# Hybrid decoder trunk on one core: inverse roots per token tile, attention low parts on VectorE, quotients and half sums behind the next piece

## The chip, the cores and the metric

The kernel runs on one core of one Trainium2 chip. The metric is device time in microseconds (us) of one execution, as the median of several runs. A core has five engines, each with an instruction queue of its own that it works off in order: PE (TensorE, the matrix products), DVE (VectorE), ACT (ScalarE), POOL (GpSimd) and SP (which here only issues transfers). An instruction that waits for another engine holds up everything behind it on its own engine.

## The reference

A batch of one, 512 tokens, 1024 channels, float32. Two layers, each followed by a SwiGLU feed-forward block: a recurrent layer (RG-LRU and Mamba-2 heads) and a layer of dilated window attention. The change touches the attention layer alone:

```python
def attention_layer(x, norm_g, w_qkv, q_norm, k_norm, w_out):
    h = rmsnorm(x, norm_g)
    qkv = (h @ w_qkv).reshape(b, l, 3, ATT_HEADS, ATT_HEAD_DIM)      # 16 heads of 64
    q = partial_rope(rmsnorm(qkv[:, :, 0], q_norm), pos) * (ATT_HEAD_DIM ** -0.5)
    k = partial_rope(rmsnorm(qkv[:, :, 1], k_norm), pos)
    v = qkv[:, :, 2]
    for window, dilation in ((128, 1), (512, 4), (2048, 16)):
        o_i, m_i, d_i = dilated_window_attention(q, k, v, window, dilation)   # softmax in a band
        ...
    # the three merged by their denominators
    return x + o @ w_out
```

`rmsnorm` of q and k is over the 64 channels of one head: each head of each token needs the inverse root of a mean square.

## The kernel before

All matrix products take float32 operands as a high part (`wh`, `xh`: rounded to fp32r) and a low part (`wl`, `xl`: what is left), three products each (low by high, high by low, high by high). `split` makes the parts: ACT casts the high part, and another engine subtracts to get the low part, DVE for most weights, POOL for those of the attention (`on_pool`: the 24 tiles of `in_w_qkv` and the 8 of `in_w_ao`). Weights come as 128x1024 tiles through three raw buffers and three pairs of parts, two weights ahead (`weight_emit`, `AHEAD`).

The attention layer works on four groups of four heads. For a group, `qk_pieces` gives 16 pieces of work for PE (4 weight tiles by 4 token tiles of 128, six matmuls each) and `v_pieces` 8 more. Pieces wait in the list `pieces`; `fill_in(n)` issues the next n of them between the small steps of the heads, so that PE has dense work while DVE and ACT prepare the next small step. After every piece, `drain(2)` issues up to two entries of a second list, `queue`: the finishing of q and k.

When the last weight tile of q and k of a token tile is done, `finish_a` copies it out of PSUM (ACT, `q`) and squares it (ACT, `qsq`). Then follow, out of `queue`, a sum over each head (DVE, L766 `qss<-qsq`, one for each token tile); once all four tiles are summed, `finish_b`: mean and epsilon (DVE, L776) and the power -0.5 on POOL for all four tiles in one instruction (L778 `qrs<-qss,mhalf`, 128x32); then `finish_c` four times (DVE, L783 `q<-q,qrs`), and the rotary part (`finish_d`, `finish_e`: `rc`, `rs`, and two sums).

The heads go in eight pairs p. For each pair: `pair_T` transposes q and k on PE and splits them (`qk_hi` ACT, `qk_lo` DVE); `scores(p, b)` for three blocks b multiplies (PE, L866 `ps_s`), adds the mask with a running maximum (DVE, L877 `s<-ps_s,cst`), takes exponentials (ACT, L878), reciprocals of the sums (DVE, L881) and the quotients (POOL, L883 `s<-s,m`); `turn` transposes the quotients (PE, L889 `ps_pT`) and splits them (`ph` ACT, `pl` DVE); `values` multiplies with v (PE, L904 and L905 `ps_o`) and at the end adds the two halves (`bot` ACT L912, `o` DVE L913) and splits `o`. The list `steps` in the loop over p sets how these alternate with pieces; the work of pair p+1's scores lies between the turns and values of pair p. The finishing of q and k of groups 1, 2 and 3 falls into pairs 0, 2 and 4.

PSUM is shared out by two pools: `pa`, four buffers for the pieces (`ps_qkv`, `ps_v`, `ps_ao`), and `pm`, three buffers for `ps_s`, `ps_pT` and `ps_qT`, beside one buffer for `ps_o`. A buffer comes free when ACT and DVE have read it. The final order on each engine is made by a scheduler from the order in the code and from when it expects operands to be ready.

Of the kernel before, what the change touches and what calls it, by code (L numbers as in the profile page):

```python
# [58 lines left out]
def trunk(ctx: ExitStack, tc: tile.TileContext, a):  # L59
# [27 lines left out]
    on_pool = ("in_w_qkv", "in_w_ao")  # L87

    def split(src, hi, lo, eng=V):
        S.copy(hi, src)  # L90
        eng.tensor_tensor(out=lo, in0=src, in1=hi.bitcast(F32), op=ALU.subtract)  # L91
# [11 lines left out]
    def weight_emit(i):  # L103
        while emitted[0] <= min(i, len(specs) - 1):
            j = emitted[0]
            src, n = specs[j]
            raw = wp.tile([P, WMAX], F32, tag="raw", bufs=NRAW, name=f"wr{j}")
            hi = wp.tile([P, WMAX], F32R, tag="whi", bufs=NSPL, name=f"wh{j}")
            lo = wp.tile([P, WMAX], F32R, tag="wlo", bufs=NSPL, name=f"wl{j}")
            step = n if j else n // 4  # L110
            for c in range(0, n, step):
                nc.sync.dma_start(out=raw[:, c:c + step], in_=src[:, c:c + step])
                split(raw[:, c:c + step], hi[:, c:c + step], lo[:, c:c + step], G if src.tensor.name in on_pool else V)
            w_of[j] = (hi, lo)
            emitted[0] += 1
# [575 lines left out]
    with ExitStack() as actx:  # L691
# [36 lines left out]
        def drain(n):  # L728
            for _ in range(min(n, len(queue))):
                queue.pop(0)()  # L730
# [3 lines left out]
        def qk_pieces(g):  # L734
            pss, sqs = [], {}

            def piece(kp, t):
                i = i_qkv[g, kp]
                if t == 0:
                    w_cur[i] = weight_get(i)  # L740
                    if kp == 0:
                        for _ in range(NT):
                            pss.append(pa.tile([P, T], F32, tag="pa", name="ps_qkv"))
                        qk[g] = at.tile([P, NT, 8, 64], F32, tag="q", name="q", bufs=2)
                        sqs["ss"] = am.tile([P, NT, 8], F32, tag="qss", name="qss")
                wh, wl = w_cur[i]
# [8 lines left out]
                if t == 1:  # L755
                    weight_emit(i + AHEAD)
# [3 lines left out]
            def finish_a(t):  # L760
# [5 lines left out]
                queue.append(lambda: V.tensor_reduce(out=sqs["ss"][:, t], in_=sq, axis=AX.X, op=ALU.add))  # L766
                if t == NT - 1:
                    queue.append(finish_b)
                    for u in range(NT):
                        queue.append(lambda u=u: finish_c(u))  # L770
                    queue.append(finish_d)
                    queue.append(finish_e)

            def finish_b():
                ss = sqs["ss"].rearrange("p t h -> p (t h)")
                V.tensor_scalar(out=ss, in0=ss, scalar1=1.0 / 64, scalar2=EPS, op0=ALU.mult, op1=ALU.add)  # L776
                rs = am.tile([P, NT, 8], F32, tag="qrs", name="qrs")
                G.tensor_tensor(out=rs.rearrange("p t h -> p (t h)"), in0=ss, in1=mhalf[:, :NT * 8], op=ALU.pow)  # L778
                sqs["rs"] = rs
# [24 lines left out]
        def v_pieces(g):  # L804
            pss = []

            def piece(vp, t):
# [15 lines left out]
                if t == 1:  # L823
# [33 lines left out]
        def scores(p, b):  # L857
# [23 lines left out]
            V.reciprocal(m[:, 2, :k], m[:, 1, :k])  # L881
            for u, s in enumerate(done):
                G.tensor_scalar(out=s, in0=s, scalar1=m[:, 2, u:u + 1], scalar2=1.0, op0=ALU.mult, op1=ALU.mult)  # L883
# [11 lines left out]
        def values(h, b):  # L895
# [17 lines left out]
            V.tensor_tensor(out=o[rows], in0=po[:64], in1=bot[rows], op=ALU.add)  # L913
            if e == 1:
                hi, lo = slot(8 + p if p < 4 else p - 4, F32R)
                split(o, hi, lo)
                oT.append((hi, lo))
# [25 lines left out]
        def fill_in(n=1):  # L943
            for _ in range(min(n, len(pieces))):
                pieces.pop(0)()
                drain(2)
# [8 lines left out]
        drain(len(queue))  # L955
# [143 lines left out]
```

## Time and profile before

| | |
|---|---|
| median of 3 runs | 1375.89 us (1375.66 to 1377.72) |
| the profiled execution, its own time | 1374.7 us |
| its span in the trace | 1372.9 us |
| PE busy | 1327.4 us, 97% of the span |
| DVE, ACT, POOL busy | 757.1, 554.1, 141.5 us |
| mean granted clock of TensorE | 0.986 |

The span runs from the first to the last instruction. PE is busy nearly all the time, so what counts is where it stands still, and where its granted clock is 0.50 in place of 1.00, which are its two levels of 1.2 and 2.4 GHz. The attention layer lies between about 717 and 1015 us of the span.

### The profile page before, as it was taken

The numbers are of one execution on the slowest core, as the hardware profiler recorded it, in microseconds if no ns is written. First come the engines' busy times: TensorE is split into PE (matmuls) and PEld (weight loads), VectorE is DVE, ScalarE is ACT, GpSimd is POOL, SyncE is SP. The second block draws the span as 40 slices with busy tenths as digits, with TensorE's granted clock in tenths as the row PEclk, the third lists the DMA queues.
The fourth block names the chain that finished last, engine by engine and source line by source line (L and its number), as shares of the span: only waits on it lengthen the run. The fifth ranks groups of instructions, "written<-read, shape, count | busy, mean of one in ns | idle before, by whom it ended". The sixth has DMA issues, their size and how long they took to land.

```text
span 1372.9 us, 15950 instructions
## 1 busy us (share of the span) xinstructions
PE 1327.4 (97%) x6314; PEld 1088.8 (79%) x6314; DVE 757.1 (55%) x1220; ACT 554.1 (40%) x818; POOL 141.5 (10%) x114
## 2 busy tenths in 40 slices
PE   8999989999999999999998889889999999999998
PEld 6877767788888888888887778777788888888887
DVE  7877799875444344444463454556564434444442
ACT  6643867443323223222343445556542322322221
POOL 0000000000000000000025344453300000000000
PEclk9999999999999999999999999989999999999999
DMA  6322223522333233333232211111123333333332
GB/s 234 109 92 77 93 77 109 152 93 92 92 102 98 92 95 101 90 100 106 81 104 93 62 47 62 47 47 47 46 93 105 95 92 96 101 92 98 106 89 81
DMA packets 38556, 126.53 MB, mean 92 GB/s; under 512 B 4289, under 2 KB 5057, under 8 KB 38353
## 3 DMA queue, kind: packets, MB, share of 16 engines
q1 hardware_dynamic: 38480, 125.51, 29.7%
q8 instruction: 49, 0.80, 0.2%
q14 instruction: 27, 0.21, 0.0%
HBM read 123.36 MB, written 2.13 MB: 91 GB/s over the span
## 4 chain that ended last, share of the span: by engine, by line
PE 87%; DVE 5%; ACT 4%; POOL 3%; issue 1%; DMA 0%; SPq 0%; ACTq 0%; POOLq 0%
PE ps_pr L119 24%; PE ps_pr L120 23%; PE ps_pr L121 23%; PE ps_qkv L752 2%; PE ps_qkv L754 2%; PE ps_qkv L753 2%; POOL qrs L778 2%; PE ps_s L866 1%; DVE q L783 1%; PE ps_pT L889 1%; POOL wl L91 1%; PE ps_o L904 1%; ACT wh L90 1%; PE ps_v L820 1%; PE ps_o L905 1%
## 5 line engine op out<-in xcount | busy, mean ns | idle before, releaser
L90 ACT CAST wh<-wr 128x1024 fp32r<-128x1024 f32 (+2 forms) x223 | 228.2, 1024 | 608.7 <-PE ps_pr L121 379.7
L119 PE MATMUL ps_pr<-xh,wl 128*128 128x512 f32 x1056 | 416.4, 394 | 12.3 <-DVE wl L91 12.0
L120 PE MATMUL ps_pr<-xl,wh 128*128 128x512 f32 x1056 | 414.3, 392 | 0.1
L121 PE MATMUL ps_pr<-xh,wh 128*128 128x512 f32 x1056 | 413.1, 391 | 0.0
L91 DVE TENSOR_TENSOR wl<-wr,wh 128x1024 fp32r<-128x1024 f32 (+2 forms) x191 | 225.9, 1184 | 53.6 <-ACT wh L90 53.2
L119 PEld LDWEIGHTS ps_pr<-xh,wl 128*128 128x128 f32 x1056 | 199.3, 189 | 54.9 <-DVE wl L91 12.8
L120 PEld LDWEIGHTS ps_pr<-xl,wh 128*128 128x128 f32 x1056 | 199.4, 189 | 43.6 <-DVE xl L194 2.0
L121 PEld LDWEIGHTS ps_pr<-xh,wh 128*128 128x128 f32 x1056 | 199.2, 189 | 41.7 <-issue 0.7
L120 PE MATMUL ps_pr<-al,wh 128*128 128x512 f32 x352 | 136.9, 389 | 0.0
L121 PE MATMUL ps_pr<-ah,wh 128*128 128x512 f32 x352 | 136.9, 389 | 0.0
L119 PE MATMUL ps_pr<-ah,wl 128*128 128x512 f32 x352 | 136.9, 389 | 0.0
L91 POOL TENSOR_TENSOR wl<-wr,wh 128x1024 fp32r<-128x1024 f32 x32 | 76.7, 2396 | 435.6 <-ACT wh L90 435.6
L673 DVE TENSOR_TENSOR tu<-ps_pr,nrb 128x512 f32<-128x512 f32 x44 | 30.4, 691 | 130.5 <-PE ps_pr L121 130.5
L681 DVE TENSOR_TENSOR x<-ps_pr,x 128x512 f32<-128x512 f32 x48 | 33.2, 692 | 120.1 <-PE ps_pr L121 119.9
L671 DVE TENSOR_TENSOR tg<-ps_pr,nrb 128x512 f32<-128x512 f32 x44 | 30.4, 691 | 94.0 <-PE ps_pr L121 94.0
L120 PEld LDWEIGHTS ps_pr<-al,wh 128*128 128x128 f32 x352 | 66.1, 188 | 13.8
L119 PEld LDWEIGHTS ps_pr<-ah,wl 128*128 128x128 f32 x352 | 66.1, 188 | 13.7
L121 PEld LDWEIGHTS ps_pr<-ah,wh 128*128 128x128 f32 x352 | 66.1, 188 | 13.6
L752 PE MATMUL ps_qkv<-wh,xl 128*128 128x512 f32 x128 | 54.3, 425 | 7.6 <-DVE v L830 7.6
L878 ACT ACTIVATE s<-s,m 128x512 f32<-128x512 f32 (+3 forms) x64 | 35.4, 554 | 54.9 <-DVE m L877 54.9
L754 PE MATMUL ps_qkv<-wh,xh 128*128 128x512 f32 x128 | 50.7, 396 | 0.0
L753 PE MATMUL ps_qkv<-wl,xh 128*128 128x512 f32 x128 | 50.6, 395 | 0.0
(231 smaller groups left out, 1671.0 us busy)
## 6 DMA issues: line engine op xcount, KB each, us to landing
wr<-in_w_gu SPq DMA_DIRECT2D x88, 512.0 KB, 3.5
wr<-in_w_in SPq DMA_DIRECT2D x35, 512.0 KB, 3.5
wr<-in_w_dn SPq DMA_DIRECT2D x32, 448.0 KB, 3.3
wr<-in_w_qkv SPq DMA_DIRECT2D x24, 512.0 KB, 3.5
wr<-in_w_out SPq DMA_DIRECT2D x16, 512.0 KB, 3.5
wr<-in_w_dn SPq DMA_DIRECT2D x16, 512.0 KB, 3.5
x<-in_xT SPq DMA_DIRECT2D x16, 256.0 KB, 3.4
bcs<-csd SPq DMA_DIRECT2D x16, 256.0 KB, 4.6
```

The costliest lines, as they stand in the source:

```text
L90: S.copy(hi, src)
L91: eng.tensor_tensor(out=lo, in0=src, in1=hi.bitcast(F32), op=ALU.subtract)
L119: mm(ps, lhsT=wl[ws], rhs=xh[xs], start=start, stop=False)
L120: mm(ps, lhsT=wh[ws], rhs=xl[xs], start=False, stop=False)
L121: mm(ps, lhsT=wh[ws], rhs=xh[xs], start=False, stop=stop)
L671: V.tensor_tensor(out=tg, in0=pg, in1=rb, op=ALU.mult)
L673: V.tensor_tensor(out=tu, in0=pu, in1=rb, op=ALU.mult)
L681: V.tensor_tensor(out=x[m], in0=ps, in1=x[m], op=ALU.add)
L752: mm(pss[t], lhsT=xl[:, ts_], rhs=wh[:, cols], start=(k == 0), stop=False)
L753: mm(pss[t], lhsT=xh[:, ts_], rhs=wl[:, cols], start=False, stop=False)
L754: mm(pss[t], lhsT=xh[:, ts_], rhs=wh[:, cols], start=False, stop=(k == KD - 1))
L878: S.activation(s, s, AF.Exp, scale=-1.0, bias=m[:, 0, u:u + 1], accum_out=m[:, 1, u:u + 1])
```

## The change

Four edits. (1) The low parts of the attention weights are made by DVE (`on_pool` goes). (2) The finishing of q and k runs by token tile: sum, mean and POOL power for one tile of 128x8, at a count of two pieces from the tile's copy (the tile's own last piece counts), and its use (`finish_c`) four pieces later; a list with counts (`later`, `tick`) takes the place of `queue` and `drain`. (3) Reciprocals and quotients of `scores`, and the half sum with its split in `values`, are put into a list that is issued behind the next piece (`after_piece`). (4) `weight_emit` inside the q, k and v pieces is called at the third token tile in place of the second.

```diff
-    on_pool = ("in_w_qkv", "in_w_ao")
-    def split(src, hi, lo, eng=V):
+    def split(src, hi, lo):
         S.copy(hi, src)
-        eng.tensor_tensor(out=lo, in0=src, in1=hi.bitcast(F32), op=ALU.subtract)
+        V.tensor_tensor(out=lo, in0=src, in1=hi.bitcast(F32), op=ALU.subtract)
...
-        def drain(n):
-            for _ in range(min(n, len(queue))):
-                queue.pop(0)()
+        after_piece = []
+        def later(n, f):
+            queue.append([n, f])
+        def tick():
+            for e in queue:
+                e[0] -= 1
+            due = [e for e in queue if e[0] <= 0]
+            queue[:] = [e for e in queue if e[0] > 0]
+            for _, f in due:
+                f()
...
-                if t == 1:
+                if t == 2:
                     weight_emit(i + AHEAD)
...
-                queue.append(lambda: V.tensor_reduce(out=sqs["ss"][:, t], in_=sq, axis=AX.X, op=ALU.add))
+                later(2, lambda: finish_b(t, sq))
+                later(6, lambda: finish_c(t))
                 if t == NT - 1:
-                    queue.append(finish_b)
-                    for u in range(NT):
-                        queue.append(lambda u=u: finish_c(u))
-                    queue.append(finish_d)
-                    queue.append(finish_e)
+                    later(7, finish_d)
+                    later(8, finish_e)
...
-            def finish_b():
-                ss = sqs["ss"].rearrange("p t h -> p (t h)")
+            def finish_b(t, sq):
+                ss = sqs["ss"][:, t]
+                V.tensor_reduce(out=ss, in_=sq, axis=AX.X, op=ALU.add)
                 V.tensor_scalar(out=ss, in0=ss, scalar1=1.0 / 64, scalar2=EPS, op0=ALU.mult, op1=ALU.add)
-                rs = am.tile([P, NT, 8], F32, tag="qrs", name="qrs")
-                G.tensor_tensor(out=rs.rearrange("p t h -> p (t h)"), in0=ss, in1=mhalf[:, :NT * 8], op=ALU.pow)
-                sqs["rs"] = rs
+                G.tensor_tensor(out=sqs["rs"][:, t], in0=ss, in1=mhalf[:, :8], op=ALU.pow)
...
-            V.reciprocal(m[:, 2, :k], m[:, 1, :k])
-            for u, s in enumerate(done):
-                G.tensor_scalar(out=s, in0=s, scalar1=m[:, 2, u:u + 1], scalar2=1.0, op0=ALU.mult, op1=ALU.mult)
+            def quotients():
+                V.reciprocal(m[:, 2, :k], m[:, 1, :k])
+                for u, s in enumerate(done):
+                    G.tensor_scalar(out=s, in0=s, scalar1=m[:, 2, u:u + 1], scalar2=1.0, op0=ALU.mult, op1=ALU.mult)
+            after_piece.append(quotients)
...
         def fill_in(n=1):
             for _ in range(min(n, len(pieces))):
                 pieces.pop(0)()
-                drain(2)
+                tick()
+            ready = after_piece[:]
+            after_piece.clear()
+            for f in ready:
+                f()
```

The half sum in `values` is wrapped the same way as `quotients` (`add`, with the split of `o` in it). Lines shift: L766, L776, L778 and L783 of before are L784, L785, L786 and L790 of the change, and L91 is L89.

How this moves instructions is seen best on DVE in pair 0, where group 1 of q and k is finished. Names: `qss` sums of squares, `q` the projected tile, `pl` low part of turned weights, `wl` low part of a weight, `o` the half sum, `ISA s,m` the scores' masked maximum. Before, DVE's queue there reads:

```order
L766 TENSOR_REDUCE qss<-qsq 128x8
L846 SCALAR_TENSOR_TENSOR qk_lo<-ps_qT,gain_5363,qk_hi 128x512
L913 TENSOR_TENSOR o<-ps_o,bot 64x512
L766 TENSOR_REDUCE qss<-qsq 128x8
L776 TENSOR_SCALAR qss<-qss 128x32
L91 TENSOR_TENSOR pl<-ps_pT,ph 128x512
L783 TENSOR_TENSOR q<-q,qrs 128x512 x4
L877 ISA s,m<-ps_s,cst 128x512
```

In the change the same stretch, from the second tile on, reads:

```order
L784 TENSOR_REDUCE qss<-qsq 128x8
L853 SCALAR_TENSOR_TENSOR qk_lo<-ps_qT,gain_5363,qk_hi 128x512
L785 TENSOR_SCALAR qss<-qss 128x8
L790 TENSOR_TENSOR q<-q,qrs 128x512
L926 TENSOR_TENSOR o<-ps_o,bot 64x512
L784 TENSOR_REDUCE qss<-qsq 128x8
L785 TENSOR_SCALAR qss<-qss 128x8
L89 TENSOR_TENSOR wl_6036<-wr_6034,wh_6035 128x1024
L89 TENSOR_TENSOR pl<-ps_pT,ph 128x512
L790 TENSOR_TENSOR q<-q,qrs 128x512
L884 ISA s,m<-ps_s,cst 128x512
```

For each tile the product `q<-q,qrs` stands directly behind the `qss<-qss` whose power POOL still has to take (for the last tile one `wl` and one `pl` lie between), and the half sum, `pl` and the scores come behind these. In pairs 2 and 4 the last part reads slightly differently: the `wl` stands ahead of the last `qss<-qss`.

On POOL, the stretch from the first to the second group before (a `wl` is a 128x1024 subtraction, `qrs` the power, `s<-s,m` quotients):

```order
L91 TENSOR_TENSOR wl_5837<-wr_5835,wh_5836 128x1024
L883 TENSOR_SCALAR s<-s,m 128x256 x2
L91 TENSOR_TENSOR wl_5898<-wr_5896,wh_5897 128x1024
L91 TENSOR_TENSOR wl_5997<-wr_5995,wh_5996 128x1024
L778 TENSOR_TENSOR qrs<-qss,mhalf 128x32
L883 TENSOR_SCALAR s<-s,m 128x512 x2
```

and in the change:

```order
L786 TENSOR_TENSOR qrs<-qss,mhalf 128x8 x4
L892 TENSOR_SCALAR s<-s,m 128x512 x2
L892 TENSOR_SCALAR s<-s,m 128x128 x2
L892 TENSOR_SCALAR s<-s,m 128x384 x2
L892 TENSOR_SCALAR s<-s,m 128x256 x2
L786 TENSOR_TENSOR qrs<-qss,mhalf 128x8 x4
```

POOL is left with powers and quotients; the 32 `wl` stand in DVE's queue. Up to pair 4, PE's and ACT's rows are the same as before, and SP's are the same throughout; in pairs 5 to 7 some rows of PE and ACT change places.

## Rows read from the trace of the kernel before

**Rows 1.** The page: engine, busy us (share of the span) and instructions.

```profile
PE 1327.4 (97%) x6314; PEld 1088.8 (79%) x6314; DVE 757.1 (55%) x1220; ACT 554.1 (40%) x818; POOL 141.5 (10%) x114
```

**Rows 2.** Waits of PE, 700 to 1000 us: total us, times, longest.

```profile
PE ps_s L866 <- DVE m L877: 16.5, 3, 5.5
PE ps_qkv L752 <- DVE v L830: 7.6, 1, 7.6
PE ps_o L904 <- DVE pl L91: 2.8, 3, 1.6
PE ps_pT L889 <- POOL s L883: 1.4, 1, 1.4
```

**Rows 3.** Windows behind the stalls: busy us by engine, granted clock, DMA share, GB/s.

```profile
759.12:762.43 3.31, 3.31 (x8) 2.64 (x9) 1.12 (x3) 0.00 (x0) 0.00 (x0) 0.50 0.00 0
803.76:810.20 6.44, 6.30 (x30) 5.67 (x31) 5.17 (x18) 5.47 (x15) 4.50 (x5) 0.50 0.02 4
...
922.36:929.60 7.24, 7.10 (x33) 6.47 (x34) 5.20 (x18) 5.82 (x16) 5.30 (x6) 0.50 0.02 6
sum 21.76, PE 21.33 PEld 18.79 DVE 16.01 ACT 15.58 POOL 12.62; mean PE 5.33 PEld 4.70 DVE 4.00 ACT 3.89 POOL 3.16
```

**Rows 4.** Timeline of POOL in pair 0: start, us, instruction.

```profile
792.78 2.39 POOL L91 TENSOR_TENSOR wl<-wr,wh 128x1024 fp32r<-128x1024 f32 x1 [7.79 <-ACT wh L90]
795.13 5.44 POOL L778 TENSOR_TENSOR qrs<-qss,mhalf 128x32 f32<-128x32 f32 x1
```

**Rows 5.** Timeline of DVE in pair 0.

```profile
789.54 0.74 DVE L846 SCALAR_TENSOR_TENSOR qk_lo<-ps_qT,gain,qk_hi 128x512 fp32r<-128x512 f32 x1
791.87 0.67 DVE L766 TENSOR_REDUCE qss<-qsq 128x8 f32<-128x512 f32 x1
792.57 0.18 DVE L776 TENSOR_SCALAR qss<-qss 128x32 f32<-128x32 f32 x1
793.34 0.69 DVE L91 TENSOR_TENSOR pl<-ps_pT,ph 128x512 fp32r<-128x512 f32 x1 [0.59 <-ACT ph L90]
800.60 2.50 DVE L783 TENSOR_TENSOR q<-q,qrs 128x512 f32<-128x512 f32 x4 [6.57 <-POOL qrs L778]
803.62 0.69 DVE L877 CUSTOM_DVE_ANT_0 s<-ps_s,cst 128x512 f32<-128x512 f32 x1
...
809.27 0.18 DVE L881 RECIPROCAL m<-m 128x4 f32<-128x4 f32 x1 [0.98 <-ACT s L878]
...
813.19 0.42 DVE L877 CUSTOM_DVE_ANT_0 s<-ps_s,cst 128x256 f32<-128x256 f32 x1
```

**Rows 6.** Timeline of PE in pair 0.

```profile
795.79 0.40 PE L904 MATMUL ps_o<-pl,v 128*128 128x512 f32 x1
803.76 1.08 PE L866 MATMUL ps_s<-qk_lo,qk_hi 64*128 64x128 f32 x2 [5.49 <-DVE m L877]
815.60 0.60 PE L889 MATMUL ps_pT<-cst,s 128*128 128x128 f32 x4
```

**Rows 7.** Timeline of DVE behind group 0.

```profile
737.41 0.69 DVE L766 TENSOR_REDUCE qss<-qsq 128x8 f32<-128x512 f32 x1 [12.58 <-ACT qsq L765]
...
749.73 6.82 DVE L783 TENSOR_TENSOR q<-q,qrs 128x512 f32<-128x512 f32 x4 [5.54 <-POOL qrs L778]
...
758.59 1.65 DVE L830 SCALAR_TENSOR_TENSOR v<-ps_v,nrt,v 128x256 fp32r<-128x256 f32 x4
```

**Rows 8.** Timeline of POOL and DVE at two powers of 128x4, earlier in the program.

```profile
295.57 1.01 POOL L220 TENSOR_TENSOR grt<-rv,mhalf 128x4 f32<-128x4 f32 x1 [49.23 <-DVE rv L218]
295.62 1.23 DVE L91 TENSOR_TENSOR wl<-wr,wh 128x1024 fp32r<-128x1024 f32 x1
362.80 2.07 POOL L220 TENSOR_TENSOR nrt<-rv,mhalf 128x4 f32<-128x4 f32 x1 [66.22 <-DVE rv L218]
362.78 1.22 DVE L91 TENSOR_TENSOR wl<-wr,wh 128x1024 fp32r<-128x1024 f32 x1
```

**Rows 9.** Timeline of DVE behind pair 5.

```profile
952.70 2.50 DVE L91 TENSOR_TENSOR xl<-o,xh 128x512 fp32r<-128x512 f32 x1 [0.70 <-ACT xh L90]
```

More of the change, by code (lines that the diff above doesn't have):

```diff
@@ L112, in weight_emit @@
                 nc.sync.dma_start(out=raw[:, c:c + step], in_=src[:, c:c + step])
-                split(raw[:, c:c + step], hi[:, c:c + step], lo[:, c:c + step], G if src.tensor.name in on_pool else V)
+                split(raw[:, c:c + step], hi[:, c:c + step], lo[:, c:c + step])
             w_of[j] = (hi, lo)
@@ L745, in piece @@
                         sqs["ss"] = am.tile([P, NT, 8], F32, tag="qss", name="qss")
+                        sqs["rs"] = am.tile([P, NT, 8], F32, tag="qrs", name="qrs")
                 wh, wl = w_cur[i]
@@ L822, in piece @@
                     mm(ps, lhsT=xh[:, ts_], rhs=wh[:, cols], start=False, stop=(k == KD - 1))
-                if t == 1:
+                if t == 2:
                     weight_emit(i + AHEAD)
@@ L912, in values, with add @@
             S.copy(bot[rows], po[64:])
[L913 to L917, printed above, removed]
+            def add():
+                V.tensor_tensor(out=o[rows], in0=po[:64], in1=bot[rows], op=ALU.add)
+                if e == 1:
+                    hi, lo = slot(8 + p if p < 4 else p - 4, F32R)
+                    split(o, hi, lo)
+                    oT.append((hi, lo))
+            after_piece.append(add)
         def ao_pieces(half, after=None):
@@ L954, in trunk @@
         fill_in(8)
-        drain(len(queue))
         pieces += qk_pieces(1)
```

## The prediction

> **What bounds the kernel now.** The page comes first: PE is busy 97% of the span, DVE 55%, POOL 10% [rows 1]. So PE's queue is the time, and the change can give back only what PE stands still or runs slowly around the attention layer. The waits of PE between 700 and 1000 us say where that is [rows 2]: 7.6 us once, in front of the first pieces of group 1, for the last readers of v (L830, DVE); three times 5.5 us in front of scores, for DVE's earlier scores; and 4.2 us in the last pairs. Together 28.3 us. The reader is to see that four of these are one event: at the end of each group of q and k, DVE stands at `q<-q,qrs` for 6.57 us [rows 5], because POOL takes the power of 32 columns in 5.44 us and starts it only behind a low part of 2.39 us [rows 4]. What PE then waits for (scores, v) stands behind that product in DVE's queue.
>
> Each stall costs a second time. Behind all four, TensorE's granted clock is 0.50, the lower of its levels; the stretches at work there add up to 21.8 us [rows 3], of which half, 10.9 us, would not be needed at the full level. That bounds the gain: 28.3 + 10.9 = 39 us, a time of 1336. The profiled execution took 1374.7 us, 1.8 more than its span and 1.2 less than the median of the runs; I sum against 1374.7 and add 1.2 at the end.
>
> **The low parts on DVE (32 tiles).** On POOL one takes 2.39 us [rows 4], on DVE 1.23 [rows 8]. POOL loses 32 x 2.39 = 76 us, DVE gets 32 x 1.23 = 39 us in some 300 us. What this removes beside POOL's time is a lock: while POOL subtracts, a DVE operation with two SBUF operands stands still. Four products of 128x512 took 6.82 us behind group 0 [rows 7] and 2.50 in pair 0 [rows 5]; one subtraction of `o` took 2.50 [rows 9]. What it adds is a place in DVE's queue. Where DVE is not held up this is covered: in pair 0 `pl` ends at 794.03 and PE uses it at 795.79 [rows 5, 6], so one low part ahead of it (1.15 from start to start) fits into 1.76 us. I cost those at nothing; two in a row, or one waiting for its cast, would not be covered.
>
> **The power by tile.** No row shows 128x8. 4 columns take 1.01 us [rows 8], 32 take 5.44 [rows 4]; the straight line gives 0.38 + 0.158 per column, so 1.64 for 8. Bounds: 1.01, and 2.7 if two halvings of 5.44 saved no more than one. I take 1.64. From the start of a mean (0.18) to the product it is then 0.18 + 1.64 + 0.1 of signals = 1.9 us. Four such waits take the place of one, and three of them are bare, because the scheduler puts the product directly behind its mean; the order shows that.
>
> **Group 0.** DVE now goes: sum, mean, wait, product, four times. A dependent mean starts 0.70 behind its sum [rows 5]; 0.70 + 1.9 + 0.62 for a product = 3.23 a tile. The first sum starts at 737.4 [rows 7], so four tiles and one low part between them (1.15) end at 751.5. The rotary part takes 2.0 (four operations between the end of the products, 756.55, and L830 at 758.59 [rows 7]), a second low part 1.15, the first v 0.41 (1.65 for four): PE can go on at 755.1 in place of 759.1 [rows 3]. That is 4.0 us. The wait of 3.6 us that is left is shorter than any of the four that pulled the clock down here, so I also take the 3.3 us at half clock [rows 3] as halved: 1.65. **5.6 us.**
>
> **Pairs 0, 2 and 4.** Pair 0 in DVE's queue, from the second `pl` at 784.4 to the end of the first block of scores, which was 804.3 [rows 5]. Work: two `pl` 1.2, a half one 0.33, four sums 2.44, two `qk_lo` 1.32, four products 2.48, the half sum 0.6, a last mean 0.1, one low part 1.15, two scores 1.3: 10.9. Waits: three bare ones, 5.7; two sums with a mean directly behind, 0.2; and the fourth. That one has the low part and a `pl` (1.75) over it, but the low part starts ahead of the power. The row at 362.80 shows what this does: a power that starts 0.02 behind such a subtraction takes 2.07 in place of 1.01 [rows 8]. So the power ends 1.5 behind the low part, and about 1.0 is bare. Sum 17.8: the scores end at 802.2, 2.1 earlier.
>
> The Trainium skill ("SBUF — State Buffer", section "SBUF: two separate sides") calls the port pair that DVE and GpSimd share an exclusive lock for whichever starts first. By that rule the low part would also wait if the power came first, and pair 0 would lose 1.7 us. The trace agrees for the subtractions on POOL and for 362.80, not for 295.62, where a low part started 0.05 behind a power and took its usual 1.23 [rows 8].
>
> What is late next: the half sum and the `pl` of the first turn now lie behind the waits, and PE's product with it, at 795.79 before [rows 6], has to wait until 799.5. So PE's stall moves 8 us forward and shrinks from 5.5 to about 3.7; then come that product, a turn and a v piece (2.25 us), and the blocked scores start at 802.3 in place of 803.76: 1.5 us. From there PE no longer sets the pace. DVE and ACT need, from the end of the scores (804.3) to the next reciprocal (809.27) 5.0 us before [rows 5], now 1.15 more for a low part; then two v, a `pl` and two scores in 2.4; then 2.0 to the transposes (813.61 to 815.60 [rows 5, 6]). 802.2 + 6.1 + 2.4 + 2.0 = 812.7 in place of 815.6: 2.9 us, nearly the same whether the clock falls or not. Before, PE in this stretch ran 6.4, 4.8 and 7.2 us at half clock in pairs 0, 2 and 4 (the sum less the other three is 4.8 [rows 3]), so the same working gives 2.9, 1.9 and 2.9. **7.7 us.** With a power of 1.01 each pair gains about 2 more, with 2.7 each loses 3 of it.
>
> **The rest.** Quotients and half sums behind the next piece: up to pair 4 the order on PE, ACT and DVE is as if they were not moved, so nothing. `weight_emit` a tile later: ACT's and SP's rows keep their order, so nothing; a tile's cast already starts when PE frees its buffer. In pairs 5 to 7 the lock on `o` (1.8 us of 2.50) and a quotient that stood behind a POOL subtraction (the 1.4 us wait [rows 2]) go, and low parts come into a queue with little slack: **1.5 us**, between -2 and +4.
>
> Sum 5.6 + 7.7 + 1.5 = 14.8: 1359.9, and 1361 on the scale of the median.
>
> **Rivals.**
> - *The waits nearly vanish.* If the power takes 1.0 and the clock stays up behind the smaller stalls, group 0 gives 8, the pairs 5 each, the last pairs 4: 27 us, 1349. For it: 1.01 at 4 columns. Against it: the slope to 32.
> - *The stall only moves.* If the power of 8 columns costs 2.3 or more, three bare waits hold DVE as long as the one did, and the blocked scores start no earlier; group 0 and the last pairs leave 0 to 3: 1373 to 1376.
> - *DVE's queue becomes the bound: slower.* Some 24 of the low parts stand ahead of something that PE waits for. Each that meets no slack costs PE 1.15, since it cannot be overtaken, and one that DVE reaches before ACT has cast its high part costs more. For it: 39 us more in the 300 of this layer are 13 points on top of DVE's 55% [rows 1], and PE's waits of up to 1.6 in the last pairs are for `pl` on DVE already [rows 2]. Against it: the 1.76 us of slack in pair 0. At full price 24 x 1.15 = 28 us against 14.8: 1389; it decides from 0.6 us for each.
>
> **How the numbers follow.** About 0.2%, 2.7 us, is what a measurement can tell here. The forecast has a chance of 0.57 (its own range, powers of 1.3 to 2.0 us: 1354 to 1368), the first rival 0.22, the second 0.08, the third 0.13. The range 1347 to 1371 leaves out the second and third rival, most of whose weight lies above 1371, and a slip of the first's lower end. Faster 0.82, same 0.06, slower 0.12.
>
> **What would show it.** A power of 128x8 at 1.6 us, four to a group; `q` and `xl` never above 0.75 us; PE's waits on L830 at about 3.6 us, and three new ones of 3 to 4 in front of `ps_o` for `pl`, in place of those in front of scores; the sum of PE's waits for scores near 2. Wrong would be: waits of PE for `wl` or `pl` all over the pairs (third rival), or powers beyond 2.3 us (second).

## The result, and the profile after

The changed kernel takes **1360.21 us**, the median of 4 runs (1359.69 to 1360.36), against 1375.78 before (4 runs, 1375.6 to 1377.72). The ratio is 0.9883, with a 95% interval of 0.9866 to 0.99: 1.2% faster. The prediction, 1361.0 with a range of 1347 to 1371, holds. The profiled execution took 1360.34 us, 1.8 over its span, as before.

The page and the waits of PE from 700 to 1000 us, which answer to [rows 1] and [rows 2] (total us, times, longest):

```profile
PE 1323.7 (97%) x6314; PEld 1086.0 (80%) x6314; DVE 779.4 (57%) x1264; ACT 553.3 (41%) x818; POOL 74.8 (6%) x94
```

```profile
PE ps_o L915 <- DVE pl L89: 10.9, 6, 3.1
PE ps_qkv L762 <- DVE v L837: 3.9, 1, 3.9
PE ps_s L873 <- DVE qk_lo L853: 1.6, 3, 0.6
PE ps_pT L900 <- POOL s L892: 0.4, 1, 0.4
```

28.3 us of waits have become 16.8. Only one kind is where it was: the wait behind group 0, 3.9 in place of 7.6. The three waits of 5.5 in front of scores are gone, and waits of 3.1 and 2.9 stand in front of `ps_o` in their place.

The stretches at half clock behind the four stalls, which answer to [rows 3] (length, PE busy with instructions, granted clock, DMA share, GB/s):

```profile
757.00:760.40 3.40, 3.40 (x10) 0.50 0.70 178
798.00:801.38 3.38, 3.38 (x20) 0.50 0.30 122
853.14:856.00 2.86, 2.86 (x11) 0.50 0.61 183
910.60:914.00 3.40, 3.40 (x18) 0.50 0.37 129
sum 13.04, PE 13.04; mean PE 3.26
```

21.8 us at half clock have become 13.0. The first row is the one to keep: 3.40 us behind group 0, where before had 3.31. Nothing was won there.

DVE, POOL and PE in pair 0, which answer to [rows 4 to 6]; each fence is the timeline of one engine (start, us, instruction, idle time ahead of it and what ended it):

```profile
790.98 0.16 DVE L785 TENSOR_SCALAR qss<-qss 128x8 f32<-128x8 f32 x1
792.89 0.69 DVE L790 TENSOR_TENSOR q<-q,qrs 128x512 f32<-128x512 f32 x1 [1.75 <-POOL qrs L786]
...
794.89 1.22 DVE L89 TENSOR_TENSOR wl<-wr,wh 128x1024 fp32r<-128x1024 f32 x1
796.03 0.68 DVE L89 TENSOR_TENSOR pl<-ps_pT,ph 128x512 fp32r<-128x512 f32 x1
797.64 0.69 DVE L790 TENSOR_TENSOR q<-q,qrs 128x512 f32<-128x512 f32 x1 [0.93 <-POOL qrs L786]
```

```profile
791.22 1.64 POOL L786 TENSOR_TENSOR qrs<-qss,mhalf 128x8 f32<-128x8 f32 x1 [2.14 <-DVE qss L785]
795.06 2.55 POOL L786 TENSOR_TENSOR qrs<-qss,mhalf 128x8 f32<-128x8 f32 x1 [2.20 <-DVE qss L785]
```

```profile
796.77 0.50 PE L915 MATMUL ps_o<-pl,v 128*128 128x512 f32 x1 [3.06 <-DVE pl L89]
```

The power starts behind its mean and DVE stands 1.75 us until it is done, three times bare; over the fourth power lie a low part and a `pl`, the low part (started 0.17 us ahead of it) makes it 2.55 long, and 0.93 is left bare. PE's `ps_o` waits for that `pl`, which stands behind the three bare waits and the low part.

All products and all roots of the layer, and the products behind group 0 with the first v ([rows 7]); a row by line gives min/median/max in ns, and the row under it who ended the idle time:

```profile
L790 DVE TENSOR_TENSOR q<-q,qrs x16: 692/693/695, 741.1 to 911.0; 128x512 f32<-128x512 f32 x16
its engine sat idle before it (us, times) until:
  POOL qrs L786: 26.1, 16
```

```profile
L786 POOL TENSOR_TENSOR qrs<-qss,mhalf x16: 1635/1636/2547, 739.5 to 909.3; 128x8 f32<-128x8 f32 x16
```

```profile
752.00 0.69 DVE L790 TENSOR_TENSOR q<-q,qrs 128x512 f32<-128x512 f32 x1 [1.75 <-POOL qrs L786]
...
755.87 1.65 DVE L837 SCALAR_TENSOR_TENSOR v<-ps_v,nrt,v 128x256 fp32r<-128x256 f32 x4
```

No product stands still for POOL any more: none takes over 0.70 us, where four took 6.82 [rows 7]; the subtractions of `o` (`xl`), one of which took 2.50 [rows 9], take 0.68 to 0.69.

**Where the time came from.** I set the starts of five PE instructions of both traces against each other: the first v piece of group 0 (739.84 before), a qk piece of group 1 behind the first stall (769.49), the first qk pieces of groups 2 (815.96) and 3 (874.89), and the 61st matmul of `ps_ao` (973.25). What is gained or lost between two of them is one stretch of this table, in us against before, with the two halves of the change alone (they are experiments below). Minus is earlier; the predicted column puts the terms for pairs 0, 2, 4 and the rest where they fall:

```
stretch                          predicted  changed  low parts on DVE alone  roots by tile alone
up to the first v of group 0        0        +0.99        +0.84                 +0.89
group 0                            -5.6      -3.67        -3.86                 +1.40
pair 0                             -2.9      -3.47        -0.73                 -2.51
pairs 1, 2                         -1.9      -2.21        -0.05                 -0.84
pairs 3 to 5, begin of output      -4.4      -5.46        -3.23                 -1.92
sum                               -14.8     -13.82        -7.03                 -2.98
```

The span got 14.4 us shorter. The last stretch can be divided at the first matmul of `ps_ao` (935.82 before, 924.12 in the change), which follows pair 4 as the first qk pieces of groups 2 and 3 follow pairs 0 and 2: 3.34 us were gained up to it, 2.12 behind it.

### The profile page after: what moved, and what is told of

Read it like the earlier page. It is cut to its first block, busy times and chain, and to the rows that moved or that the text cites. A ratio compares the mean times of both kernels' runs of the same rounds, so it can differ in the third digit from the quotient of the medians.

```text
span 1358.5 us, 16006 instructions
## 1 busy us (share of the span) xinstructions
PE 1323.7 (97%) x6314; PEld 1086.0 (80%) x6314; DVE 779.4 (57%) x1264; ACT 553.3 (41%) x818; POOL 74.8 (6%) x94
## 4 chain that ended last, share of the span: by engine, by line
PE 86%; DVE 6%; ACT 4%; POOL 2%; issue 1%; DMA 0%; SPq 0%; POOLq 0%; ACTq 0%; DVEq 0%
PE ps_pr L117 24%; PE ps_pr L118 24%; PE ps_pr L119 24%; PE ps_qkv L762 2%; POOL qrs L786 2%; PE ps_qkv L764 2%; PE ps_qkv L763 2%; PE ps_ao L119 1%; PE ps_ao L117 1%; PE ps_ao L118 1%; DVE wl L89 1%; PE ps_s L873 1%; PE ps_pT L900 1%; ACT s L885 1%; DVE qss L784 1%
## 5 line engine op out<-in xcount | busy, mean ns | idle before, releaser
L89 DVE TENSOR_TENSOR wl<-wr,wh 128x1024 fp32r<-128x1024 f32 (+2 forms) x223 | 265.3, 1190 | 76.4 <-ACT wh L88 75.6
L892 POOL TENSOR_SCALAR s<-s,m 128x512 f32<-128x512 f32 (+3 forms) x64 | 38.4, 616 | 109.9 <-DVE m L890 84.4
```

The source lines that it names most:

```text
L89: V.tensor_tensor(out=lo, in0=src, in1=hi.bitcast(F32), op=ALU.subtract)
```

## Experiments

Medians of each kernel and of before in the same runs, ratio with 95% interval:

```
kernel                                       us       before    ratio (interval)
low parts on DVE alone                     1367.71   1375.61   0.9939 (0.9924 to 0.9954)
roots by tile, low parts on POOL           1370.72   1375.61   0.9961 (0.9946 to 0.9976)
quotients and half sums at once            1359.68   1375.61   0.9883 (0.9867 to 0.99)
no power (roots left out)                  1337.20   1375.61   0.9719 (0.9705 to 0.9733)
every power twice                          1384.16   1376.41   1.0057 (1.0042 to 1.0072)
every low part twice                       1350.55   1376.41   0.9814 (0.9799 to 0.9829)
unread matmuls at four places              1363.30   1376.41   0.9906 (0.989 to 0.9923)
unread matmuls behind group 0              1358.82   1376.61   0.9873 (0.9859 to 0.9886)
one mean for two tiles                     1350.08   1376.61   0.9811 (0.9798 to 0.9824)
roots by Newton steps on DVE               1342.76   1376.41   0.9759 (0.9744 to 0.9773)
the same, every low part twice             1347.28   1376.61   0.9789 (0.9776 to 0.9803)
Newton, two steps for three                1343.91   1376.10   0.9766 (0.9752 to 0.9779)
```

**My theory:** two causes, a POOL that is free of low parts (no lock, no power queued behind a subtraction) and smaller powers; what is left is DVE standing at its products. **Rivals:** all of the gain is from one of the two; the later quotients have a share; DVE's load is by now what costs.

### The low parts alone

The kernel before, with

```diff
-    on_pool = ("in_w_qkv", "in_w_ao")
+    on_pool = ()
```

> The kernel before, with one part of the change alone: the low parts of the attention weights on DVE. The power stays one of 128x32 per group. My theory (the gain has two sources, a POOL that is free when the power is due, and smaller powers): the power starts some 2.3 us earlier in the pairs, where a low part on POOL no longer stands ahead of it; the four products of group 0 take 2.5 us in place of 6.82; one or two low parts more stand in DVE's queue. That is 4.3 for group 0, 1.2 to 2.4 for each of three pairs and 1.5 for the last pairs: 1363 to 1367. Rival A, all of the gain comes from this part: 1359 to 1361. Rival B, all of it comes from the inverse roots by tile: 1374 to 1377.

It took 1367.71, half of the gain and 0.7 above my range. PE's waits, and pair 0 on DVE and POOL:

```profile
PE ps_o L904 <- DVE pl L91: 17.9, 6, 5.3
PE ps_qkv L752 <- DVE v L830: 3.9, 1, 3.9
```

```profile
789.73 1.23 DVE L91 TENSOR_TENSOR wl<-wr,wh 128x1024 fp32r<-128x1024 f32 x1
...
796.28 1.29 DVE L783 TENSOR_TENSOR q<-q,qrs 128x512 f32<-128x512 f32 x2 [5.33 <-POOL qrs L778]
```

```profile
789.83 6.42 POOL L778 TENSOR_TENSOR qrs<-qss,mhalf 128x32 f32<-128x32 f32 x1 [11.94 <-DVE qss L776]
```

Behind group 0 the wait is 3.9, that of the full change: there the low parts are the whole gain. In the pairs PE still waits up to 5.3. The power does start directly behind its mean, as I expected, but beside a low part that DVE began 0.10 us earlier it takes 6.42 in place of 5.43, so that 1.0 of the 2.4 us saved ahead of it is lost again.

### The roots by tile alone

The changed kernel with the low parts back on POOL (`eng.tensor_tensor` with `on_pool` as before).

> The changed kernel with the low parts of the attention weights back on POOL; the roots by tile, the later quotients and half sums stay. My theory: each of the four powers of a group can now stand behind a subtraction of 2.4 us, and DVE's products and sums stand still while POOL subtracts, so that what the small powers save is lost again at some tiles: 1367 to 1375. Rival A (all from the low parts on DVE): 1374 to 1377 or more. Rival B (all from the roots by tile): 1359 to 1362.

It took 1370.72, 4.9 less than before by the medians (the profiled executions, which the table goes by, are 3.0 apart). PE's waits, and one product of group 0 beside what POOL did then:

```profile
PE ps_o L917 <- DVE pl L91: 15.0, 6, 4.1
PE ps_qkv L764 <- DVE v L839: 7.9, 1, 7.9
```

```profile
747.43 2.88 DVE L792 TENSOR_TENSOR q<-q,qrs 128x512 f32<-128x512 f32 x1 [1.75 <-POOL qrs L788]
```

```profile
747.36 2.40 POOL L91 TENSOR_TENSOR wl<-wr,wh 128x1024 fp32r<-128x1024 f32 x1
```

Group 0 gets nothing from the roots by tile: four bare waits of 1.75 hold DVE longer than the one of 5.5 did, and two products that meet a subtraction on POOL take 2.88 and 2.82 for 0.69. The pairs get most of theirs, 2.51 of 3.47 in pair 0. So neither rival holds; both parts are needed, each for another place.

### Quotients and half sums at once

The changed kernel with its third part undone (`quotients()` and `add()` called where they were queued, `weight_emit` at `t == 1`).

> The changed kernel with its third part undone: quotients and half sums are issued at once, and the next weight tile at token tile 1. My theory, as predicted, costs this part at nothing: 1359 to 1361.5, and the waits of PE between 700 and 1000 us as in the changed kernel. A rival gives it a share of the gain: 1363 or more, with a wait of POOL's or DVE's that stands ahead of a score or of a high part's reader. If the 1.5 us that PE now waits for a high part at the start of the attention layer, or near it, go away, the order of the weight tiles made them.

1359.68, and PE's waits for `pl`, v and `qk_lo` are those of the changed kernel to the tenth (10.9, 3.9 and 1.6 us). The third part is worth nothing, as costed.

### No power at all

```diff
-                V.tensor_scalar(out=ss, in0=ss, scalar1=1.0 / 64, scalar2=EPS, op0=ALU.mult, op1=ALU.add)
-                G.tensor_tensor(out=sqs["rs"][:, t], in0=ss, in1=mhalf[:, :8], op=ALU.pow)
+                V.tensor_scalar(out=sqs["rs"][:, t], in0=ss, scalar1=1.0 / 64, scalar2=EPS, op0=ALU.mult, op1=ALU.add)
```

> The changed kernel without the power on POOL: the mean goes where the inverse root stood, and the product reads it at once, so the inverse root of the q and k rows is left out of the computation. My theory (what is left of PE's stalls in group 0 and pairs 0, 2 and 4 is DVE standing 1.75 us before each product): the waits of 3.9 and three times 2.9 us and the stretches at half clock behind them go, 12.7 of waits and some 6.8 of clock, of which a little comes back as waits for scores: 1341 to 1346. Rival: DVE's queue is the bound there by now (low parts ahead of what PE waits for), so waits of 2 us or more and their stretches at half clock stay: 1350 to 1357.

This kernel leaves the inverse roots out; DVE's order in the layer stays as it is but for two means. It took 1337.20, below what I expected: PE waits 1.6 us in all from 700 to 1000 us, in place of 16.8, and the clock is 1.00 throughout. That is the whole price of the powers as they now stand: 23 us. DVE has as many instructions as in the changed kernel, so its load isn't what limits.

```profile
PE ps_o L914 <- DVE pl L89: 1.6, 3, 1.0
```

### Every power twice

The line with `ALU.pow` a second time.

> The changed kernel with every power of q and k taken twice, one after the other into the same columns: each tile's inverse root comes 1.64 us later, and DVE has no more to do. My theory (three of four waits of a group are bare, since a product stands directly behind its mean): group 0 loses 4 times 1.64, 6.6 us, pairs 0, 2 and 4 lose 3 times 1.64 each, 14.8 together, and the longer stalls bring some more at half clock: 1378 to 1385. Rival: the waits overlap with work that is due anyway, and a later root costs at most its last wait, 1.64 for a group: 1363 to 1368.

1384.16, slower than before. DVE's waits for roots grow by 22.2 us, of the 26.2 that 16 more powers of 1.64 take:

```profile
  POOL qrs L787: 48.3, 16
```

Against the changed kernel group 0 loses 7.1 us (6.6 expected) and pairs 1, 2 4.7 (4.9); pair 0 loses 6.9, two more than three bare waits, which I did not follow up. A longer root is hardly covered anywhere.

### Every low part twice

```diff
+                if src.tensor.name in ("in_w_qkv", "in_w_ao"):
+                    V.tensor_tensor(out=lo[:, c:c + step], in0=raw[:, c:c + step], in1=hi[:, c:c + step].bitcast(F32), op=ALU.subtract)
```

> The changed kernel with every low part of the attention weights taken twice on DVE: 32 operations of 1.2 us more in some 300 us. My theory: a low part costs PE something only where it stands ahead of what PE waits for (the two behind the products of group 0, the one ahead of the pl of pairs 0, 2 and 4, one or two in the last pairs), 7 to 9 times 1.15: 1366 to 1371. The prediction's third rival (most of them stand ahead of something that PE waits for): 24 times 1.15 or more, 1385 to 1395. DVE's load costs nothing at all: 1360 to 1362.

None of these: **1350.55**, 9.7 us faster than the changed kernel with 32 operations more. The reason is in DVE's rows of pair 0. The scheduler, with other work to place, had put other instructions between the means and the products:

```profile
787.26 0.69 DVE L794 TENSOR_TENSOR q<-q,qrs 128x512 f32<-128x512 f32 x1 [0.43 <-POOL qrs L790]
788.86 0.69 DVE L794 TENSOR_TENSOR q<-q,qrs 128x512 f32<-128x512 f32 x1 [0.91 <-POOL qrs L790]
...
792.47 1.21 DVE L115 TENSOR_TENSOR wl<-wr,wh 128x1024 fp32r<-128x1024 f32 x1
...
795.21 0.69 DVE L794 TENSOR_TENSOR q<-q,qrs 128x512 f32<-128x512 f32 x1 [0.31 <-POOL qrs L790]
```

The waits of 1.75 have become 0.3 to 1.2, with three powers of the same 1.64 and one of 3.14. Over the layer DVE stands 10.4 us for roots, in place of 26.1. So this run didn't price a low part; it suggests that the order of DVE's queue is worth more than 32 further low parts cost. Two runs below separate the two: one mean for two tiles, and the price of a low part.

### One mean for two tiles

The changed kernel; the sums stay by tile, and `finish_b` is called for tiles 1 and 3 alone:

```diff
+            def finish_b(t):
+                ss = sqs["ss"][:, t - 1:t + 1]
+                V.tensor_scalar(out=ss, in0=ss, scalar1=1.0 / 64, scalar2=EPS, op0=ALU.mult, op1=ALU.add)
+                for u in (t - 1, t):
+                    G.tensor_tensor(out=sqs["rs"][:, u], in0=sqs["ss"][:, u], in1=mhalf[:, :8], op=ALU.pow)
```

> The changed kernel with the same four powers of 128x8 per group, but with one mean for two tiles: two sums, one mean of 128x16, two powers, two products. No operation gets shorter; only the order on DVE differs: a product no longer stands directly behind a sum and mean of its own. My theory (what is left of the stalls is the bare wait of a product behind its own mean, and the run with doubled low parts was faster because its order had fewer of those): DVE's waits for inverse roots fall from 26.1 us to 10 to 16, the stalls in pairs 0, 2 and 4 fall below 1.5 us, the clock stays up behind them: 1346 to 1353. Rival: that order was not what made it faster, and the waits of 1.75 us are covered or merely move: 1358 to 1362.

**1350.08**, as the theory had it. The same 16 powers, and DVE's waits for them are 15.6 us:

```profile
  POOL qrs L791: 15.6, 13
```

Pair 0 gains 5.37 over before in place of 3.47, group 0 7.23 in place of 3.67, and the longest wait of PE in front of `ps_o` is 1.0. No operation is shorter. Eight means of 0.16 us fall away, little of the 10 us; what is different is what stands between a mean and its product. The step of the prediction "three of them are bare, because the scheduler puts the product directly behind its mean" was thus the place where 10 of the 23 us that the powers still cost could be had.

### The roots on DVE

A mean of 128x32 per group, and in place of the power a first guess from its bits and three Newton steps:

```diff
+                V.tensor_scalar(out=g0, in0=ss.bitcast(I32), scalar1=-0.5, scalar2=1597463007.0, op0=ALU.mult, op1=ALU.add)
+                z = g0.bitcast(F32)
+                for _ in range(3):
+                    V.tensor_tensor(out=w, in0=z, in1=z, op=ALU.mult)
+                    V.scalar_tensor_tensor(out=w, in0=w, scalar=-0.5, in1=ss, op0=ALU.mult, op1=ALU.mult)
+                    V.scalar_tensor_tensor(out=y, in0=w, scalar=1.5, in1=z, op0=ALU.add, op1=ALU.mult)
+                    z = y
```

> The changed kernel with the inverse roots of q and k on DVE: a first guess from the bits of the mean and three Newton steps, once per group on 128x32, eleven small operations and no power on POOL. My theory (PE's stalls in the attention layer are DVE waiting for POOL, not DVE's load): eleven dependent operations of 0.15 to 0.25 us are 1.7 to 2.8 us per group, some 9 in all, without a wait for another engine; the stalls go as in the run without the power, which took 1337.2, and a part of the 9 comes back in front of the first products with a low part: 1338 to 1345, faster than both kernels. Rival: the chain stands in DVE's queue ahead of what PE waits for and costs as much as the four waits of 1.75 us: 1348 to 1360.

**1342.76**, the fastest of those that compute the roots, 2.4% below the kernel before. The chain on DVE behind group 0 (its mean, its last step and the first product):

```profile
744.31 0.18 DVE L791 TENSOR_SCALAR qss<-qss 128x32 f32<-128x32 f32 x1
...
746.55 0.19 DVE L798 SCALAR_TENSOR_TENSOR qrs<-qw,qrs 128x32 f32<-128x32 f32 x1
746.78 2.49 DVE L803 TENSOR_TENSOR q<-q,qrs 128x512 f32<-128x512 f32 x4
```

From the mean to the products are 2.5 us for 32 columns, where POOL alone took 5.44 [rows 4]. What is late next is a quotient of POOL: `ps_pT` waits 3.1 us in four times, and `ps_o` 1.2.

With two steps in place of three, the first with fitted constants:

> The version with the inverse roots on DVE with two Newton steps in place of three; the first step's constants are set so that two are enough for the accuracy of fp32. Three small operations fewer per group; in the run with three steps each took 0.19 us and stood 0.225 from the next. My theory (behind a group the chain stands on DVE ahead of the product of a turn, pl, which PE is short of): 3 times 0.225, 0.7 us, for each of three pairs at most, nothing in group 0, where PE no longer waits: 1340.5 to 1342.5. Rival: the chain is covered everywhere by now: 1342.5 to 1343.5, no change.

1343.91, just above both ranges: three operations fewer in a group bring nothing that the times can tell, so the chain is covered.

### The price of a low part

The Newton version with every low part twice, the same edit as above.

> The kernel with the inverse roots by Newton steps on DVE, which took 1342.8, with every low part of the attention weights taken twice: 32 operations of 1.2 us more on DVE, and no wait for POOL whose place in the order could change with them. This prices the load that the change puts on DVE. My theory (DVE has slack nearly everywhere in this layer): 0 to 7 us, 1343 to 1350. The prediction's third rival (most of the 32 stand ahead of something that PE waits for): 24 times 1.15, 1370 or more. In between, 1351 to 1369, would mean that a low part costs 0.3 to 0.8 us on average, so that the 32 of the change itself gave back a good part of its gain.

1347.28, 4.5 us more than 1342.76: **0.14 us for each of 32**, where one takes 1.2 on DVE. Here no product waits for a power, and the edit costs a little; in the changed kernel the same edit gave 9.7. Together they say that the run with doubled low parts was faster by its order. The 0.14 is an average, since the order shifts here too: pair 0 gains 8.14 over before, where the Newton version alone gains 6.92, and the other stretches gain less than there. PE's waits for quotients are 6.9 us in place of 3.1:

```profile
PE ps_pT L917 <- POOL s L909: 6.9, 5, 1.7
```

### TensorE kept busy in the stalls

Matmuls of 128x512 into a bank that the next real matmul overwrites: 13 on v ahead of group 1's first piece, 10 ahead of the first `ps_o` of pairs 0, 2 and 4.

```diff
+        def warm(p, po, n):
+            v = vt[p // 2, 0]
+            for _ in range(n):
+                mm(po, lhsT=v[:, 0].rearrange("p a e -> p (a e)"), rhs=v.rearrange("p h a e -> p (h a e)"), start=True, stop=True)
```

> The changed kernel with matmuls that nobody reads where PE would stand still: 13 of 128x512 (0.24 us each) ahead of the first piece of group 1 and 10 ahead of the first ps_o of pairs 0, 2 and 4. They end before the wait that they stand in does. If TensorE's clock falls because PE stands still, the granted clock stays at 1.0 behind these four places, and half of four stretches of 3.4 us comes back: 1353 to 1357. Rival: the clock falls for another reason (what PE does before or behind the stall), and the stretches at half clock stay: 1360 to 1363. If the matmuls are longer than the waits, each place costs the difference, up to 1 us.

1363.30: slower, and not as either theory had it. Two of my placements were wrong, and the timeline of PE shows both:

```profile
757.45 4.83 PE L909 MATMUL ps_w<-v 128*128 128x512 f32 x13 [3.89 <-DVE v L837]
...
786.63 2.43 PE L909 MATMUL ps_o<-v 128*128 128x512 f32 x10
```

Behind group 0 they read what PE was waiting for, stood behind the wait and made the next real piece 4.7 us later, 2.95 over the whole stretch. In the pairs they stood ten microseconds ahead of the stall (which is at the second head of the pair, 796.77 above). Still they tell something: PE comes to the stall 2.4 us later, waits at most 0.6 there, and the granted clock stays at 1.00 through all three pairs; in pair 0, behind the stall (length, PE busy, granted clock, DMA share, GB/s):

```profile
800.78:806.00 5.22, 5.22 (x41) 1.00 0.35 104
```

Yet the stretches of the table come out as in the changed kernel: -3.47 for pair 0, -2.35 for pairs 1 and 2, -5.61 for the rest. What the faster clock gives back PE loses again in short waits, in the three pairs six for `pl` and three for a quotient, of up to 0.6. So **in the pairs the clock costs nothing**: behind the stall it isn't PE that sets the pace.

The second try, behind group 0 alone: 12 matmuls on the last high part of x, which has long been there.

> The changed kernel with 12 matmuls of 128x512 that nobody reads, on data that has long been there, in the wait of 3.87 us behind group 0; the earlier try read v, which is what PE waits for there, and so stood behind the wait. They take 2.8 to 2.9 us and end a microsecond before the wait does. If the clock falls because PE stands still, the granted clock is 1.00 from 756 to 762 us, and 1.7 us come back: 1358 to 1359. Rival: the stretch of 3.4 us at 0.50 stays there: 1360 to 1361. The granted clock in the trace decides, since 1.7 us are about what the times can tell.

1358.82, 1.4 less than the changed kernel. The windows around the wait (length, PE busy, granted clock, DMA share, GB/s) and PE's first piece behind it:

```profile
754.00:756.00 2.00, 1.39 (x7) 1.00 0.00 0
756.00:758.00 2.00, 1.47 (x6) 1.00 0.37 86
758.00:760.00 2.00, 2.00 (x13) 1.00 0.62 193
```

```profile
756.53 0.50 PE L762 MATMUL ps_qkv<-wh,xl 128*128 128x512 f32 x1 [1.14 <-DVE v L837]
```

The clock stays at 1.00, and group 0's stretch is -5.25 in place of -3.67: 1.58 us, the size that the prediction had for it, but had taken for granted.

This run also says the same of the pairs, without a matmul added there. In pair 2 PE waited 2.92 us, as in the changed kernel, but the clock stayed at 1.00 behind it, where the changed kernel has 2.86 us at 0.50:

```profile
851.68 0.50 PE L915 MATMUL ps_o<-pl,v 128*128 128x512 f32 x1 [2.92 <-DVE pl L89]
```

```profile
851.68:858.00 6.32, 6.09 (x48) 1.00 0.29 86
```

PE runs up to 1.3 us ahead on the way and is level again at the first piece of group 3: the stretch of pairs 1 and 2 is -2.22, against -2.21 with the slow clock.

## Why the prediction was right, step by step

The time came out 0.8 us from the forecast, and the mechanism is the one described. That it came so close is in part luck: group 0 gave 1.9 us less than its term and the start of the program came 1.0 us later, while the pairs and the end gave 1.9 more.

- **The power of 128x8**: 1.64 taken, 1.635 to 1.636 measured, 2.55 beside a low part. The 0.93 left bare behind the fourth is the "about 1.0" of the working. That the two ends of the line (4 and 32 columns) gave 8 so well carried everything else.
- **Group 0, 5.6 forecast, 3.67 measured.** The wait was right: PE stands 3.89 us (3.6 forecast). The step that failed is "so I also take the 3.3 us at half clock as halved: 1.65". Behind the wait of 3.89 the clock was 0.50 just as behind 7.6, for 3.40 us at work against 3.31 [rows 3]. The unread matmuls show that 1.58 was there to be had where the clock stays up. Nor did the working say which half of the change this gain belongs to: it is the low parts', and the roots by tile alone make group 0 longer by 1.40. The 6.57 us that the prediction gives for all four events are the pairs'; behind group 0 DVE stood 5.54 [rows 7], and its products 6.82.
- **Pair 0 and its like, 2.9 and 1.9 forecast, 3.47 and 2.21 measured.** The place of the new stall is exact: `ps_o` at 796.77, which is 799.44 on the scale of before (PE comes to this pair 2.67 earlier), was forecast for 799.5. The wait is 3.06 (3.7 forecast). The blocked scores start at 802.98 on that scale, not at 802.3 (the working's own terms, 799.5 and 2.25, give 801.8), and the rest of the chain is shorter than summed. "Nearly the same whether the clock falls or not" is shown by the run whose clock didn't fall in any pair, and by pair 2 of the run with unread matmuls behind group 0 alone: both gained the same.
- **The rest**: 2.9 forecast for pair 4, 3.34 measured; 1.5 forecast for what is behind, 2.12 measured.
- **Quotients, half sums, weight tiles**: nothing, as costed.
- **Up to group 0** both halves and the whole lose 0.8 to 1.0 us, which the sum doesn't have. The same stretch is 0.3 to 2.1 us later over all kernels here, 1.13 and 2.05 in the two with unread matmuls, which are the changed kernel up to there. The change has no visible part in it: up to 708 us the instructions of PE, DVE, ACT and POOL are the same in both traces, and of the 0.99 us, 0.83 are there at the 101st matmul of the first products (`ps_pr`, 38.56 before, 39.39).

**The rivals.** *DVE's queue becomes the bound* needed 0.6 us for each of 24 low parts; 32 further ones cost 0.14 each in the Newton version. *The waits nearly vanish* is what taking the power away gives, 1337 and less than the 1349 I had for it. It doesn't even need a power of 1.0: with powers of 1.64 and one mean for two tiles the waits in front of `ps_o` are at most 1.0 and the time is 1350. What the rival had wrong was its condition, the length of the power in place of the order. *The stall only moves* was priced too low: powers of twice 1.64 didn't give 1373 to 1376 but 1384, since hardly any of a longer root is covered.

The Trainium skill's exclusive lock ("SBUF — State Buffer", section "SBUF: two separate sides") gives the port pair that DVE and GpSimd share to whichever instruction starts first, for its whole length. It is half borne out: a product that met a subtraction on POOL took 2.88 us, but a power that had started first did not hold DVE up (below).

## What to carry to other kernels

A small root on a slow engine costs its latency at every place where the scheduler puts the consumer directly behind the producer: count the bare waits in the order of the waiting engine before counting work, since here the order was worth 10 us and 32 more operations of 1.2 us only 4.5. A short chain on the engine that waits (2.5 us for a group) beat four calls of 1.64 us to another engine. A half-clock stretch is only worth its time where PE sets the pace behind it: find out which engine ends the stretch first.

## What the runs showed of the hardware

- **A power on POOL that started first doesn't hold DVE up; a subtraction does.** In all traces here together, 64 low parts and products of q and k began on DVE 0.05 to 0.9 us into a power with no low part ahead of it, and each took its usual time, as at 295.57 [rows 8]. In the run with doubled low parts the product at 787.26 (row above) took 0.69 inside the second of these two powers, and the two together no more than 3.24:

```profile
785.59 3.24 POOL L790 TENSOR_TENSOR qrs<-qss,mhalf 128x8 f32<-128x8 f32 x2 [0.89 <-DVE qss L789]
```

  In a single one of the 64 cases the power was longer: it began at 792.03, a low part in the middle of it at 792.47 took its 1.21 (row above), and the power 3.14 in place of 1.64. Why only there stays open.

```profile
792.03 3.14 POOL L790 TENSOR_TENSOR qrs<-qss,mhalf 128x8 f32<-128x8 f32 x1 [3.21 <-DVE qss L789]
```

  Behind a low part that DVE had begun 0.10 to 0.17 us earlier a power of 128x8 took 2.55 in place of 1.64, and one of 128x32 6.42 in place of 5.43. A subtraction on POOL that started 0.07 ahead of a product did hold DVE up (2.88 for 0.69). POOL was first in both kinds of rows; what differs is its operation.
- **The length of a wait alone doesn't decide about the clock.** In the changed kernel PE waited 2.92 us up to 853.14, and the clock was 0.50 behind it (window above). In the run with unread matmuls behind group 0 it waited as long for the same instruction, and the clock stayed at 1.00 (851.68, above); two pairs later, after 2.92 us again, it was 0.50. In the run with doubled low parts it waited 2.92 us behind group 0, and the clock stayed:

```profile
755.72 0.50 PE L766 MATMUL ps_qkv<-wh,xl 128*128 128x512 f32 x1 [2.92 <-DVE v L841]
```

```profile
756.00:758.00 2.00, 2.00 (x9) 1.00 0.23 16
758.00:760.00 2.00, 2.00 (x14) 1.00 0.64 246
```

  What else counts I did not find out.
